# Six gate strips of layer 1 as block products in pairs, in a two-layer encoder trunk

## The chip, the cores and the metric

The kernel runs on one core of one Trainium2 chip. Its time is the device time of one execution in microseconds (us). The engines are TensorE (PE, its weight loads PEld), VectorE (DVE), ScalarE (ACT), GpSimd (POOL), and SyncE (SP), which issues nearly all DMAs from one queue in program order.

## What is computed

A trunk of two layers over 1024 tokens of width 1024. Layer 0 is differential attention, layer 1 latent attention (MLA), each with adaptive norm, a gate path `silu(z)` and a gated residual. Of the reference, what bears on the change:

```python
shift, scale, gate = _modulation(c, ada_w[i], ada_b[i])   # silu(c) @ ada_w + ada_b, in three
h = _rmsnorm(x, norm_g[i]) * (1.0 + scale) + shift
...
proj = h @ w_in                                            # layer 1
q_a, c_kv, k_pe, z = jnp.split(proj, [384, 640, 704], axis=-1)
q = (_rmsnorm(q_a, q_a_norm_g) @ w_q_b)                    # 8 heads x (128 + 64)
kv = (_rmsnorm(c_kv, kv_a_norm_g) @ w_kv_b)                # 8 heads x (128 + 128): k_nope, v
q_pe, k_pe = rope(...)
sc = (qn @ k_nope.T + qp @ k_pe.T) * scale
o = softmax(sc) @ v
o = o * silu(z)
x = x + gate * (o @ w_out)
```

z is 1024 wide: eight strips of 128 columns, one for each head.

## The kernel before

Activations lie transposed: 128 features on the partitions, 512 tokens (a half) in a row, so h1, the input of layer 1, is eight blocks k of two halves. Every operand is split into a high part (fp32r) and the rest, and each product is three matmuls (`mm3`, L178 to L180): hi x hi, lo x hi, hi x lo.

A strip (128 output columns) takes its weights as two raw tiles (`wraw`, two buffers, 256 KB each), has them split by a cast on ScalarE (L223, `wh`) and a subtraction on GpSimd (L224, `wl`), and runs two halves of 8 blocks x 3 matmuls into an accumulator of PSUM (`acc`, two buffers). Layer 1 runs 14 strips of `w_s1`: the rope part of the keys, three for q_a, two for c_kv (`lora`), then eight gate strips z (`z1_strip`). The blocks of h1 for half 0 and half 1 are made by `h_chunk` (a transposition trh on TensorE, L487 on ScalarE, L491 and L492 on VectorE), those of half 1 from a list `side`, of which one entry runs per block step of a strip.

`lora` keeps the raw strips in `craw`, sums their squares (`csum`, L1237), and `norm` adds the sums over partitions by four small matmuls (`cps`, L1242), takes the inverse root, broadcasts it through memory (`bc_s`), and scales (L1251); the results CQ and CK (hi and lo, 20 tiles) stay in SBUF. The parts of a norm are queued in `norms` and run in the next half's fifth block step.

A gate half goes from `acc` through tanh on ScalarE (L705, `zth`) and a product on VectorE (L706, `gz`) to memory, `zS`. Amid the gate strips stand eight dot products on VectorE (L428, 128x1024) of ada rows of 512 KB each, which make layer 1's gate vector.

Then come the v tiles (`v1_tile`): 16 products of CK with `wv` into `vps`, evacuated by ScalarE and VectorE as `v_hl` (L355, L356), and written to `vS` by DMAs of 512 KB. Among them stand the first strips of `stream1`, made from CQ and CK: `qr` (rope part of the queries, through `rp_sw` DMAs), `kn` and `qn`. The first scores (L1397) need all of these. Attention 1 runs head by head: scores, the maximum (L393, `nm`), exp (L395), transpositions `tr` (L376) with their two parts `pth` (ScalarE, L378) and `ptl` (VectorE, L379), and the products with v (`pv`).

The order of the instructions within an engine is a scheduler's, from the program's order and priorities.

Of the kernel before, what the change touches and what calls it, by code (L numbers as in the profile page):

```python
# [21 lines left out]
P = 128  # L22
# [56 lines left out]
def f32v(ap):  # L79
    return ap.bitcast(F32)  # L80
# [3 lines left out]
def trunk(ctx: ExitStack, tc: tile.TileContext, A, out):  # L84
# [325 lines left out]
    def mod_load(src, mp, nb, tag="ada"):  # L410
        w = mp.tile([P, D], F32, name="ada", tag=tag, bufs=nb)
        SP.dma_start(w, src)
        return w
# [56 lines left out]
                else:  # L470
                    V.tensor_scalar(piece, piece, y[:, j : j + 1], None, op0=ALU.mult)

    def h_chunk(l, xn4, k, dst, hp, sub=G, wide=False, act=False):

        _, _, _, a_, b_ = mods[l]
        if wide:
            tr = bank("cb", "trc", [P, D])[:, :HF].rearrange("p (j q) -> p j q", j=4)
        else:
            tr = bank("tr", "trh", [P, 4, P])
        for j in range(len(xn4)):  # L480
            nk = KT // len(xn4[j])
            PE.transpose(tr[:, j, :], xn4[j][k // nk][:, (k % nk) * P : (k % nk + 1) * P], ident)
        n = len(xn4)
        hh, hl = dst
        ak, bk = a_[:, k : k + 1], b_[:, k : k + 1]
        tmp = hp.tile([P, n, P], F32, name="h32", tag="h32", bufs=2)
        S.activation(hh, tr[:, :n, :], AF.Identity, bias=bk, scale=ak)  # L487
        if act:
            S.activation(tmp, tr[:, :n, :], AF.Identity, bias=bk, scale=ak)
        else:  # L490
            V.tensor_scalar(tmp, tr[:, :n, :], ak, bk, op0=ALU.mult, op1=ALU.add)  # L491
        return sub.tensor_sub(hl, tmp, f32v(hh)).ins  # L492
# [668 lines left out]
    w4 = []  # L1161

    def strip1(i, wpool=None):
        return load_strip([A["w_s1"][i, f] for f in range(2)], [4, 4], wpool)
# [1 line left out]
    def group0(gi, fulls):  # L1166
        fulls = [[x_] for x_ in fulls]
        norm_x(ss1[gi], fulls, (2, 3) if gi else ())

        def chunk(k):  # L1170
            if gi == 1:
                h1[k][1] = xt2k("h1h"), xt2k("h1l")
            h_chunk(1, fulls, k, h1[k][gi], p3x, V)
# [14 lines left out]


    stC = ExitStack()  # L1190
    cqp = pool(stC, "cq", side="right")
    CQ = [[(cqp.tile([P, HF], F32R, name=f"cqh{k}_{f}"), cqp.tile([P, HF], F32R, name=f"cql{k}_{f}")) for f in range(2)] for k in range(3)]
    CK = [[(cqp.tile([P, HF], F32R, name=f"ckh{k}_{f}"), cqp.tile([P, HF], F32R, name=f"ckl{k}_{f}")) for f in range(2)] for k in range(2)]
# [4 lines left out]
    st4 = ExitStack()  # L1198

    def kp_half(half, acc):  # L1200
        rot, fin = rope(wp, acc, half, 1.0)

        def g():
            rot()
            r = fin()
            hi = lr.tile([P, HF], F32R, name="kp_h", tag="kp_h", bufs=1)
# [4 lines left out]
        return g  # L1211

    norms = []

    def half_and_norm(w, half, consume):

        for k, _ in enumerate(gen_half(w, h1, half, consume)):
            if k == NORM_AT:
                for f in norms[:]:
                    norms.remove(f)  # L1220
                    f()

    def lora(idx, dst, gvec, width, ws=None, first=None):
        n = len(idx)
        craw = [[None, None] for _ in range(n)]
        sums = [None, None]
        def put(i, half, acc):
            t = lr.tile([P, HF], F32, name="craw", tag="craw", bufs=6)
            S.copy(t, acc)
            craw[i][half] = t  # L1230
            if i == 0:
                sums[half] = lr.tile([P, HF], F32, name="csum", tag="csum", bufs=2)
                S.activation(sums[half], acc, AF.Square)
            else:
                s2 = lr.tile([P, HF], F32, name="csq", tag="csq", bufs=1)
                S.activation(s2, acc, AF.Square)
                V.tensor_add(sums[half], sums[half], s2)  # L1237

        def norm(half):
            pt = bank("tr", "cps", [P, 4, P])  # L1240
            for j in range(4):
                PE.matmul(pt[:, 0, j : j + 1], sums[half][:, j * P : (j + 1) * P], ones[:, 0:1], start=True, stop=True)  # L1242
# [3 lines left out]
            _, rb = bcast_rows(lr, y, "cbc", 1)  # L1246
# [22 lines left out]
    def first_halves(put):  # L1269

        g0 = kp_half(0, strip_half(w4[0], h1, 0))
        for _ in gen_half(w4[1], h1, 0, put):
            side.tick()
        side.flush()
        st3x.close()
        g0()
        kp_half(1, strip_half(w4[0], h1, 1))()

    lora((1, 2, 3), CQ, qag, QL, w4[1], first_halves)
    lora((4, 5), CK, kvg, KVL)  # L1280

    def z1_strip(h, extra=None):
        w = strip1(6 + h)
        if extra:
            extra()
        for half in range(2):
            def put(acc, half=half):
                gz = silu_gate(wp, acc)
                SP.dma_start(zS[h, half], gz)
            half_and_norm(w, half, put)  # L1290

    z1_strip(0)
    stL.close()
    stv = ExitStack()
    pv1 = pool(stv, "pv1", side="right")
    p4 = pool(st4, "p4")

    c2, c_fin = load_c(p4, p4.tile([P, D], F32, name="cth", tag="ada", bufs=2))
    c_fin()
    gates = gen_gate(1, lambda src: mod_load(src, p4, 2), c2)  # L1300
    next(gates)
    wk = [[None, None] for _ in range(2)]

    def load_wk(fh, wpool):
        for k in range(2):
            raw = p4.tile([P, HF], F32, name="wvr", tag="wvr", bufs=2)
            SP.dma_start(raw, A["w_v1"][k, fh])
            h_ = wpool.tile([P, HF], F32R, name="wvh", tag="wv1", bufs=4)
            l_ = wpool.tile([P, HF], F32R, name="wvl", tag="wv1", bufs=4)
# [12 lines left out]
    for h in range(1, NH):  # L1322
        next(gates)
        z1_strip(h, lambda: [load_wk(fh, wpool) for fh, wpool in enumerate((p4, pv1))] if h == NH - 1 else None)
    for tt in range(NT):
        v1_tile(tt, 0, p4)
    st4.close()
    sth.close()

# [44 lines left out]
    for h in range(NH):  # L1374
# [4 lines left out]
    stream1 = Stream(gen_strips(items))  # L1379

    def scores1(h, half, ti, zz):

# [21 lines left out]
    def attn1(h, fills, extra=None, late=None):  # L1404
# [5 lines left out]
        def close(half, o_, zz):  # L1410
            if late and half == 1:
                ctx_["late"] = late(o_, zz, ctx_["gz"])
                return
            o = ap.tile([P, HF], F32, name="o1", tag="o", bufs=2)
            V.scalar_tensor_tensor(out=o, in0=o_, scalar=0.5, in1=ctx_["gz"], op0=ALU.mult, op1=ALU.mult)
            V.reciprocal(zz, zz)
            finish(o, zz, 1, h, half, None, ap, None)

        ctx_ = dict(pool=ap, l=1, h=h, open=open_, close=close)
        for qp in range(4):  # L1420
# [37 lines left out]
    for tt in v1_left:  # L1458
        v1_tile(tt, 1, ap, "pt", 6)
    stv.close()  # L1460
    for h in range(NH - 1):
        attn1(h, lambda i: FILL1[i])
        while late_q:
            late_q.pop(0)()
        stream1.step(sum(steps1[: h + 2]) - stream1.count)
    stw.close()
    stC.close()
    stO = ExitStack()
# [158 lines left out]
```

## Time and profile before

| what | value |
|---|---|
| median of 3 runs | 1448.29 us (1446.67 to 1448.92) |
| the profiled execution | 1448.22 us |
| its span | 1446.4 us |
| VectorE, instructions | 1272 |
| ScalarE / GpSimd, instructions | 1258 / 484 |
| layer 1's strips | 781 to 949 us |
| v tiles, to the first scores | 949 to 986 us |
| attention 1 | about 1000 to 1360 us |

The page gives an engine's busy time, its share of the span and its instructions. A row of the timeline has start, duration, engine, line, operation, output and inputs, shapes, and in brackets how long the engine had been idle and who released it. A row of the waits names who waited for whom: total, times and longest. A row of the windows has for each engine the busy time and instructions, then the granted TensorE clock (1.00 is full), the share of DMA and its rate.

### The profile page before, as it was taken

To read this page: it belongs to the slowest core of one execution; us is meant where nothing else is said; L and a number is where in the kernel's file an instruction comes from. 1 tells how busy PE (TensorE), PEld (TensorE's weight loads), DVE (VectorE), ACT (ScalarE), POOL (GpSimd) and SP (SyncE) were. 2 spreads that over 40 slices of the span, in tenths; PEclk is the share of its full clock that TensorE was granted. 3 is DMA by queue.
4 is the path that set the end of the run, shared out by engine and by line. 5 is a ranking of instruction groups with operands and counts; after the bars stand their busy time and mean duration, and the time that the engine had idled before them with its cause. 6 is when DMAs were issued, how large, how long until landed. Compare 5 with 4: busy or idle time off the path is not lost.

```text
span 1446.4 us, 20456 instructions
## 1 busy us (share of the span) xinstructions
PE 1396.9 (97%) x7424; PEld 1167.0 (81%) x7424; DVE 858.4 (59%) x1272; ACT 710.5 (49%) x1258; POOL 605.0 (42%) x484
## 2 busy tenths in 40 slices
PE   5999999999999999998999999998999999999997
PEld 4778788888888887887787878787888888888886
DVE  6656777767777767677344445134555555555365
ACT  5522366656565665566343332234454554545342
POOL 4416164656564655453551264321141321412473
PEclk9999999999999999999999999999999999999999
DMA  9787823333333324137653127367242332345574
GB/s 327 234 248 234 256 66 97 87 103 81 101 97 88 98 81 110 63 95 262 229 171 124 38 69 239 110 189 204 77 104 77 110 99 76 105 136 175 172 238 149
DMA packets 128470, 203.19 MB, mean 140 GB/s; under 512 B 18289, under 2 KB 55281, under 8 KB 128369
## 3 DMA queue, kind: packets, MB, share of 16 engines
q1 hardware_dynamic: 128368, 201.89, 45.6%
q8 instruction: 58, 0.95, 0.3%
q14 instruction: 44, 0.35, 0.1%
HBM read 132.68 MB, written 45.56 MB: 123 GB/s over the span
## 4 chain that ended last, share of the span: by engine, by line
PE 77%; DMA 7%; DVE 6%; ACT 3%; POOL 3%; issue 2%; SPq 2%; ACTq 0%; DVEq 0%; POOLq 0%
PE s L1397 10%; PE acc L180 8%; PE acc L179 8%; PE acc L178 8%; PE tr L376 7%; PE s L767 7%; PE pv L179 4%; PE pv L178 4%; PE pv L180 4%; PE oacc L178 4%; PE oacc L179 4%; PE oacc L180 4%; DMA ada<-in_ada_g 2%; DMA wvr<-in_w_v 2%; DMA vS<-v_hl 1%
## 5 line engine op out<-in xcount | busy, mean ns | idle before, releaser
L378 ACT CAST pth<-tr 128x512 fp32r<-128x512 f32 x256 | 150.3, 587 | 283.6 <-PE tr L376 280.0
L393 DVE TENSOR_REDUCE nm<-s 128x1 f32<-128x1024 f32 x192 | 234.0, 1219 | 73.6 <-PE s L767 64.0
L379 DVE TENSOR_TENSOR ptl<-tr,pth 128x512 fp32r<-128x512 f32 x256 | 176.2, 688 | 150.2 <-ACT pth L378 149.9
L224 POOL TENSOR_TENSOR wl<-wraw,wh 128x512 fp32r<-128x512 f32 (+2 forms) x94 | 116.8, 1244 | 243.4 <-ACT wh L223 216.2
L395 ACT ACTIVATE e<-s,nm 128x1024 f32<-128x1024 f32 x128 | 143.7, 1122 | 28.1 <-DVE nm L393 27.6
L376 PE MATMUL tr<-ident,e 128*128 128x128 f32 x1024 | 154.6, 273 | 1.9 <-DVE ptl L379 1.7
L376 PEld LDWEIGHTS tr<-ident,e 128*128 128x128 f32 x1024 | 121.5, 140 | 42.8 <-DVE ptl L379 19.2
L178 PE MATMUL acc<-h0h,wh 128*128 128x512 f32 x360 | 150.0, 417 | 2.0 <-DVE v_hl L356 1.9
L178 PE MATMUL pv<-pth,vt 128*128 128x256 f32 x512 | 147.4, 288 | 0.0
L179 PE MATMUL pv<-ptl,vt 128*128 128x256 f32 x512 | 145.5, 284 | 0.0
L180 PE MATMUL pv<-pth,vt 128*128 128x256 f32 x512 | 144.6, 282 | 0.0
L180 PE MATMUL acc<-h0h,wl 128*128 128x512 f32 x360 | 142.2, 395 | 0.5 <-POOL wl L224 0.5
L179 PE MATMUL acc<-h0l,wh 128*128 128x512 f32 x360 | 141.4, 393 | 0.0
L1007 POOL TENSOR_TENSOR wol<-wor,woh 128x512 fp32r<-128x512 f32 x64 | 85.8, 1361 | 84.4 <-ACT woh L1006 79.4
L178 PEld LDWEIGHTS pv<-pth,vt 128*128 128x128 f32 x512 | 97.6, 191 | 3.0 <-ACT pth L378 0.4
L179 PEld LDWEIGHTS pv<-ptl,vt 128*128 128x128 f32 x512 | 97.7, 191 | 2.6
L180 PEld LDWEIGHTS pv<-pth,vt 128*128 128x128 f32 x512 | 97.7, 191 | 0.1
L325 POOL TENSOR_TENSOR rp_sw<-rp_sw,sinT 128x512 f32<-128x512 f32 x42 | 55.2, 1314 | 80.6 <-DMA rp_sw<-rp_raw 77.6
L767 PE MATMUL s<-ks,qa 128*128 128x512 f32 x256 | 82.2, 402 | 3.5 <-DVE e L775 3.1
L775 DVE SCALAR_TENSOR_TENSOR e<-s,z,e 128x1024 f32<-128x1024 f32 x64 | 82.1, 1283 | 2.1
L223 ACT CAST wh<-wraw 128x512 fp32r<-128x512 f32 (+2 forms) x94 | 55.2, 587 | 55.8 <-PE acc L179 38.5
L320 POOL TENSOR_TENSOR rp_r<-rp_raw,cosT 128x512 f32<-128x512 f32 x38 | 49.4, 1302 | 78.5 <-ACT rp_raw L315 50.8
(469 smaller groups left out, 3281.7 us busy)
## 6 DMA issues: line engine op xcount, KB each, us to landing
wraw<-in_w_s SPq DMA_DIRECT2D x76, 256.0 KB, 2.8
ada<-in_ada_ss SPq DMA_DIRECT2D x32, 512.0 KB, 6.1
vS<-v_hl SPq DMA_DIRECT2D x32, 512.0 KB, 4.9
vt<-vS SPq DMA_DIRECT2D x32, 512.0 KB, 4.0
wor<-in_w_out SPq DMA_DIRECT2D x64, 256.0 KB, 3.9
rp_sw<-rp_raw SPq DMA_DIRECT2D x168, 64.0 KB, 2.0
bc_s<-bc_d SPq DMA_DIRECT2D x34, 256.0 KB, 4.0
ada<-in_ada_g SPq DMA_DIRECT2D x16, 512.0 KB, 5.2
```

Source lines behind the costliest of these rows:

```text
L178: PE.matmul(psum, ah, bh, start=first, stop=False)
L179: PE.matmul(psum, ah, bl, start=False, stop=False)
L180: PE.matmul(psum, al, bh, start=False, stop=last)
L224: sub = (V if pair_of else G).tensor_sub(l_[:, :n], raw[:, :n], f32v(h_[:, :n]))
L376: PE.transpose(tr[:, j, :], p[:, kt * P : (kt + 1) * P], ident)
L378: mk["S"] = S.copy(pth[kh][:, :, dst], tr).ins
L379: mk["V"] = V.tensor_sub(ptl[kh][:, :, dst], tr, f32v(pth[kh][:, :, dst])).ins
L393: mk["V"] = V.reduce_max(nm, s_ps, axis=AX.X, negate=True).ins
L395: mk["S"] = S.activation(e, s_ps, AF.Exp, bias=nm, scale=1.0, accum_out=zs).ins
L767: PE.matmul(s_ps[:, kc * HF : (kc + 1) * HF], src[:, c, ql], KS[h][kc][:, c, :], start=fst, stop=not fst)
L1007: in_turn(G.tensor_sub(lo, raw, f32v(hi)))
L1397: PE.matmul(s_ps[:, kc * HF : (kc + 1) * HF], lhs, rhs(kc), start=i == 0, stop=i == 4)
```

## The change

The gate strips 0 and 1 stay as they were. Strips 2 to 7 are taken in pairs (`z_pair`). The pair's weights are a 2 x 2 matrix of blocks (strip m, half f of the features), h1 a 2 x 2 matrix (blocks k and k + 4, half of the tokens), and the four blocks of the result come from seven products of 4 blocks x 3 matmuls (`product`, accumulator `zacc`), instead of eight, with sums ahead of and behind them:

- `combos` makes T1 to T4 of h1 on VectorE: for each k four combinations, 6 additions or subtractions and 4 subtractions for the low parts, and 4 casts on ScalarE. They are entries of `side`. h1's half 1 is kept in f32 (`h1f`) for it, and its chunks come in the order 0, 4, 1, 5, 2, 6, 3, 7.
- `z_weights` makes four sums of raw weights per pair on VectorE and splits seven tiles (ScalarE, GpSimd); raw weights come into six buffers `zraw`.
- `z_pair` adds the products up on VectorE (`zu`, `zu3`, one copy on ScalarE), with tanh and gate product as before.

For the room in SBUF, CQ and CK are written to memory (`cS`, 20 tiles of 256 KB) when they are made, and loaded again (`load_ck`) in the last pair, when T2, T3 and T1 come free. The gate vector's dot products move into attention 1 (`gate_steps`), as 16 halves of 512, with loads of 256 KB. The first `qr` weights are fetched and split ahead of the v tiles.

The core of the diff:

```diff
@@ group0 / lora
-            side.add(*[lambda k=k: chunk(k) for k in range(KT)])
+        side.add(*[lambda k=k: chunk(k) for k in ((0, 4, 1, 5, 2, 6, 3, 7) if gi else range(KT))])
...
-                    hi, lo = dst[i][half]
+                    pl, tag = (wp, "rp") if dst else (p4, "zraw")
+                    hi = pl.tile([P, HF], F32R, name="c_h", tag=tag, bufs=6)
                     S.copy(hi, t)
-                    G.tensor_sub(lo, t, f32v(hi))
-
+                    G.tensor_sub(t.bitcast(F32R), t, f32v(hi))
+                    his.append(hi)
+                norms.append(store)
+
+            def store():
+                for i in range(n):
+                    SP.dma_start(cS[dst + i, half, 0], f32v(his[i]))
+                    SP.dma_start(cS[dst + i, half, 1], craw[i][half])
@@ combos
+        for k in range(4):
+            (ah, al), (bh, bl) = h1[k][0], h1[k + 4][0]
+            c_, d_ = h1f[k], h1f[k + 4]
+            t1 = tmp4("t1")
+            V.tensor_sub(t1, c_, f32v(ah))
+            V.tensor_sub(t1, t1, f32v(al))
+            split_t(1, k, t1, t1d[k])
+            yield
+            t2 = tmp4("t2")
+            V.tensor_sub(t2, d_, t1)
+            split_t(2, k, t2, t2d[k])
+            yield
+            t4 = tmp4("t4f")
+            V.tensor_sub(t4, f32v(bh), t2)
+            V.tensor_add(t4, t4, f32v(bl))
...
+            t3_ = tmp4("t3")
+            V.tensor_sub(t3_, d_, c_)
+            split_t(3, k, t3_, (ut("t3h"), ut("t3l")))
+            yield
@@ first_halves
+        cg = combos()
+        for _ in range(16):
+            side.add(None, None, lambda: next(cg), None, None)
@@ z_weights
+            s1 = p4.tile([P, HF], F32, name="zs1", tag="zraw", bufs=6)
+            V.tensor_add(s1, a21, a22)
+            V.tensor_sub(a21, a11, a21)
+            V.tensor_sub(a11, s1, a11)
+            V.tensor_sub(a12, a12, a11)
+            for t in (a11, a21, s1, a22, a12):
+                yield split_raw(t, 4)
@@ z_pair
+        S.copy(u, product(h1q(0, 0)))
+        acc = product(h1q(1, 0))
+        c_ = rpt("z11")
+        V.tensor_add(c_, acc, u)
+        gate_out(2 * p, 0, c_, c_)
+        V.tensor_add(u, product(TC[2]), u)
+        late(0)
...
+        acc = product(TC[3])
+        u3 = rpt("zu3")
+        V.tensor_add(u3, acc, u)
+        late(1)
+        acc = product(TC[1])
+        c_ = rpt("z22")
+        V.tensor_add(c_, acc, u3)
+        V.tensor_add(u, acc, u)
+        gate_out(2 * p + 1, 1, c_, c_)
+        late(2)
...
+        V.tensor_add(u3, product(TC[4]), u3)
+        gate_out(2 * p + 1, 0, u3, u3)
+        V.tensor_add(u, product(h1q(1, 1)), u)
+        gate_out(2 * p, 1, u, u)
@@ late_z
+        if i == 0:
+            load_ck(CK, 3, [(k, half) for half in range(2) for k in range(2)])
...
+        if i == 2:
+            load_wk(0)
+            load_ck(CQ, 0, [(i, half) for half in range(2) for i in range(3)])
+    z_pair(1)
+    load_wk(1)
+    z_pair(2)
+    z_pair(3, late_z)
+    wqr0 = split_strip(kraw)
@@ gate_steps
+        for j in range(KT):
+            yield
+            for i in range(2):
+                SP.dma_start(gw[i], A["ada_g1"][j, :, i * HF : i * HF + HF])
+            yield
+            yield
+            js = slice(j, j + 1)
+            for i in range(2):
+                with behind("V"):
+                    mod_dot(gw[i], part("ada_bg1")[:, js] if i == 0 else gcol1[:, js], gcol1[:, js], cg2[i])
@@ attention 1
-        attn1(h, lambda i: FILL1[i])
+        attn1(h, lambda i: FILL1[i], lambda i: next(gate1, None))
```

How the instructions stand. On VectorE, where h1's last blocks of half 1 and the first csum are made, before:

```order
L491 TENSOR_SCALAR h_7955<-trh,moda_92,modb_93 128x512
L492 TENSOR_TENSOR h1l<-h_7955,h1h 128x512
L491 TENSOR_SCALAR h_7969<-trh,moda_92,modb_93 128x512
L492 TENSOR_TENSOR h1l<-h_7969,h1h 128x512
L491 TENSOR_SCALAR h_7987<-trh,moda_92,modb_93 128x512
L492 TENSOR_TENSOR h1l<-h_7987,h1h 128x512
L329 TENSOR_TENSOR rp_r<-rp_r,rp_sw 128x512
L1237 TENSOR_TENSOR csum<-csum,csq 128x512
```

The same place in the change (t_8008 and t_8028 are T1 and T2 of k = 0, t4f its T4):

```order
L491 TENSOR_SCALAR h1f_7931<-trh,moda_92,modb_93 128x512
L492 TENSOR_TENSOR h1l<-h1f_7931,h1h 128x512
L1243 TENSOR_TENSOR t_8008<-h1f_7861,h_0h 128x512
L491 TENSOR_SCALAR h1f_7945<-trh,moda_92,modb_93 128x512
L1244 TENSOR_TENSOR t_8008<-t_8008,h_0l 128x512
L492 TENSOR_TENSOR h1l<-h1f_7945,h1h 128x512
L1248 TENSOR_TENSOR t_8028<-h1f_7875,t_8008 128x512
L491 TENSOR_SCALAR h1f_7963<-trh,moda_92,modb_93 128x512
L1252 TENSOR_TENSOR t4f<-h_4h,t_8028 128x512
L492 TENSOR_TENSOR h1l<-h1f_7963,h1h 128x512
L1228 TENSOR_TENSOR t1l<-t_8008,t1h 128x512
```

Four combinations have moved in ahead of the last h1l; the others follow, and csum stands among them.

On SP, at the passage from the gate strips to the v tiles, before:

```order
L202 DMA wraw<-in_w_kn 128x256
L202 DMA wraw<-in_w_qn 128x384
L1408 DMA gz_9534<-zS 128x512
L1289 DMA zS<-gz 128x512
L358 DMA vS_0_71<-v_hl 256x4x128 x8
L319 DMA rp_sw<-rp_raw 32x512 x8
```

And in the change, from the last loads of CQ (L1462) on:

```order
L1462 DMA ckh<-cS 128x512
L1462 DMA ckl<-cS 128x512
L1395 DMA zS<-zu_9149 128x512
L1395 DMA zS<-zu 128x512
L358 DMA vS_0_71<-v_hl 256x4x128 x8
L202 DMA wraw<-in_w_kn 128x256
L319 DMA rp_sw<-rp_raw 32x512 x4
L202 DMA wraw<-in_w_qn 128x384
L319 DMA rp_sw<-rp_raw 32x512 x4
```

The loads from cS stand ahead of the eight vS writes, and the kn and qn weights now behind them.

On VectorE in attention 1, head 0, second half, in the change:

```order
L379 TENSOR_TENSOR ptl<-tr,pth 128x4x128
L428 ISA gwh,gcol<-gwh,c2h,vec 128x512
L428 ISA gcol 128x1
L428 ISA gwh,gcol<-gwh,c2h,gcol 128x512
L428 ISA gcol 128x1
L379 TENSOR_TENSOR ptl<-tr,pth 128x4x128
L393 TENSOR_REDUCE nm<-s_9905 128x1
L1539 SCALAR_TENSOR_TENSOR qn_l<-acc,qn_h 128x512
```

A pair of dot products and their reads stands between two ptl; before, two ptl followed each other there.

More of the change, by code (lines that the diff above doesn't have):

```diff
@@ L1190, in trunk, with ut @@
     stC = ExitStack()
[L1191 to L1193 removed]
+    up = pool(stC, "u", side="right")
+    def ut(name, spare=False, dt=F32R):
+        return up.tile([P, HF], dt, name=name, tag="us" if spare else "u", bufs=4 if spare else 20)
+    TC = {}
+    cS = dr.tile([5, 2, 2, P, HF], F32, name="cS")
     stw = ExitStack()
@@ L1295, in trunk, with z_weights @@
     pv1 = pool(stv, "pv1", side="right")
[L1296 to L1301, printed above, removed]
+    def z_weights():
+        for _ in range(1, NH // 2):
+            a11, a12 = zraw[:2]
+            yield split_raw(a11, 4)
+            yield split_raw(a12, 4)
+            a21, a22 = zraw[2:4]
+            del zraw[:4]
+            s1 = p4.tile([P, HF], F32, name="zs1", tag="zraw", bufs=6)
[5 more added lines that the diff above has]
+                yield split_raw(t, 4)
@@ new lines, in gate_out, with product @@
+    def gate_out(h, half, c_, dst):
+        th = wst.tile([P, HF], F32, name="zth", tag="gz", bufs=3)
+        S.activation(th, c_, AF.Tanh, scale=0.5)
+        V.scalar_tensor_tensor(out=dst, in0=th, scalar=1.0, in1=c_, op0=ALU.add, op1=ALU.mult)
+        SP.dma_start(zS[h, half], dst)
+    zw = z_weights()
+    zq = [next(zw), next(zw)]
+    def product(rhs):
+        hi, lo = zq.pop(0)
+        zq.append(next(zw, None))
+        acc = bank("acc", "zacc")
+        for k in range(4):
+            mm3(acc, hi[k], lo[k], *rhs[k], k == 0, k == 3)
+        return acc
@@ L1320, in v1_tile, with load_ck, late_z @@
         store_v(1, sp, acc, tt, fh, *buf)
-    for h in range(1, NH):
-        next(gates)
-        z1_strip(h, lambda: [load_wk(fh, wpool) for fh, wpool in enumerate((p4, pv1))] if h == NH - 1 else None)
+    CK, CQ = [[None, None] for _ in range(2)], [[None, None] for _ in range(3)]
+    def load_ck(dst, n0, order):
+        for i, half in order:
+            dst[i][half] = ut("ckh"), ut("ckl")
+            for j, t in enumerate(dst[i][half]):
+                SP.dma_start(f32v(t), cS[n0 + i, half, j])
+    kraw = []
+    def late_z(i):
+        if i == 0:
+            load_ck(CK, 3, [(k, half) for half in range(2) for k in range(2)])
+            raw = p4.tile([P, HF], F32, name="zraw", tag="zraw", bufs=6)
+            SP.dma_start(raw[:, : 3 * P], A["w_qr"][0])
+            kraw.append((raw, 3))
+        if i == 2:
[6 more added lines that the diff above has]
+    wqr0 = split_strip(kraw)
+    st4.close()
+    p4 = pool(st4, "p4v")
     for tt in range(NT):
```

114 lines of the change are left out of this document (87 added, 27 removed).

## The prediction

> **What bounds the kernel now.** I read the page's engine row first, then the waits of TensorE around the changed stage, then that stage cut into pieces of 20 us.
>
> ```profile
> PE 1396.9 (97%) x7424; PEld 1167.0 (81%) x7424; DVE 858.4 (59%) x1272; ACT 710.5 (49%) x1258; POOL 605.0 (42%) x484
> ```
>
> TensorE is busy for 97% of the span, so a matmul that goes is worth its own time wherever TensorE doesn't wait. The waits between 780 and 1000 us, the stretch that the change rewrites (columns: total, times, longest):
>
> ```profile
> PE vps L178 <- DVE qn_l L1349: 4.4, 1, 4.4
> PE acc L180 <- POOL wl L224: 1.5, 1, 1.5
> PE trh L482 <- DVE xfull L471: 1.5, 2, 0.8
> PE cps L1242 <- DVE csum L1237: 1.1, 1, 1.1
> ```
>
> That is 8.5 us in all. The same stretch by pieces (columns: PE, PEld, DVE, ACT, POOL busy, granted clock, DMA share, GB/s):
>
> ```profile
> 781.00:858.00 77.00, 74.36 (x347) 59.57 (x346) 35.42 (x47) 31.82 (x53) 30.99 (x23) 1.00 0.23 72
> 858.00:949.00 91.00, 89.46 (x392) 72.60 (x391) 29.93 (x42) 22.18 (x38) 32.13 (x25) 1.00 0.48 155
> 949.00:966.00 17.00, 17.00 (x75) 13.78 (x74) 6.22 (x9) 6.73 (x13) 1.17 (x2) 1.00 0.84 244
> 980.00:1000.00 20.00, 17.29 (x69) 13.91 (x70) 8.85 (x13) 8.90 (x16) 2.52 (x2) 0.83 0.86 245
> ```
>
> In the strips (781 to 949) TensorE is the bound, the other engines have half their time free, and DMA is light. In the v tiles (from 949) DMA is the busy resource. After 1000 us TensorE again works alone:
>
> ```profile
> 1000.00:1360.00 360.00, 359.53 (x2187) 308.64 (x2186) 191.59 (x257) 184.56 (x335) 99.19 (x80) 1.00 0.37 108
> ```
>
> The profiled execution took 1448.22 us (span 1446.4 and 1.8 outside it); the median of the runs is 1448.29, so sums made on the one hold for the other.
>
> **The change part by part.**
>
> *The products.* A plain strip is 2 halves x 8 blocks x 3 = 48 matmuls of 128x512, a pair 96. The pair by seven products is 7 x 4 x 3 = 84. Three pairs: 36 matmuls fewer. Their price comes from ScalarE's tanh of the second halves, three strips apart:
>
> ```profile
> 916.59 0.59 ACT L705 ACTIVATE zth<-acc 128x512 f32<-128x512 f32 x1
> ...
> 949.66 0.59 ACT L705 ACTIVATE zth<-acc 128x512 f32<-128x512 f32 x1
> ```
>
> 33.07 us for 144 matmuls is 0.2297 us each; 36 of them are **-8.3 us**. What would eat this is a product that comes late. Each lasts 12 x 0.2297 = 2.76 us. VectorE has per pair 4 sums of weights, 7 sums of products and 4 gate products, 15 x 0.69 = 10.4 us in 19.3 us, of which before's gz products were already some. ScalarE has 7 weight casts, a copy and 4 tanh at 0.6 us, GpSimd 7 weight subtractions of about 1.3 us. All stay near half load, and the scheduler puts the weights' sums two products ahead. I cost the inside of a product at nothing; one product held up by 0.5 us at each pair's start would cost 1.5.
>
> *The raw weights.* The 1.5 us wait for wl follows from weights that landed late:
>
> ```profile
> ACT wh L223 <- DMA wraw<-in_w_s: 8.6, 3, 3.3
> L428 DVE CUSTOM_DVE_ANT_0 ada<-ada,c,vec 128x1024 f32<-128x1024 f32 x8 | 11.6, 1450 | 10.8 <-DMA ada<-in_ada_g 10.8
> ```
>
> The eight ada loads of 512 KB, amid which these weights were fetched, leave the stage with their dot products: **-1.5** (between 0 and -1.5; the weights now come through a ring of six buffers, so I take the end).
>
> *h1's combinations.* They add 40 VectorE instructions and 16 casts between the last h1 chunks and the end of the k strips. A 128x512 VectorE instruction is 0.69 us, so 27.6 us more on an engine with 35.4 of 77 us: 63 of 77 us. It fits as a mean, and not where TensorE waits in order for VectorE. Two such places exist. Four of the combinations now stand ahead of the last chunk's h1l:
>
> ```profile
> 806.98 0.81 DVE L491 TENSOR_SCALAR h<-trh,moda,modb 128x512 f32<-128x512 f32 x1
> 807.82 0.69 DVE L492 TENSOR_TENSOR h1l<-h,h1h 128x512 fp32r<-128x512 f32 x1
> 816.11 0.69 DVE L329 TENSOR_TENSOR rp_r<-rp_r,rp_sw 128x512 f32<-128x512 f32 x1 [7.60 <-POOL rp_sw L325]
> ```
>
> This h1l is 4 x 0.69 = 2.8 us later, and the 7.6 us of idle behind it become the combinations' place. The other is the four norms' csum, which cps on TensorE waits for:
>
> ```profile
> 827.64 0.69 DVE L1237 TENSOR_TENSOR csum<-csum,csq 128x512 f32<-128x512 f32 x1 [4.37 <-ACT csq L1236]
> 834.38 0.90 DVE L1237 TENSOR_TENSOR csum<-csum,csq 128x512 f32<-128x512 f32 x1 [3.49 <-ACT csq L1236]
> ```
>
> VectorE was idle when these came; now up to three combinations (2.1 us) can stand ahead of each. The norm stands 4 blocks into the next half (12 matmuls, 2.8 us), which hid all but 1.1 us of one. Bounds: 0, and 2.8 + 4 x 2.1 = 11. Nearest row is the 1.1 us wait, behind three scalings of 4.40 us in all; I take about twice that, **+2**.
>
> *Normalized c through memory.* CQ and CK are written to cS (20 x 256 KB, in a stretch with DMA at 0.23 to 0.48) and read back late: 8 loads after the third product of the last pair, 8 after the fourth, 4 after the fifth, because only then are T2, T3 and T1 free. That is 5.2 MB and four zS writes, 6.3 MB, starting 4 x 2.76 = 11 us ahead of the v tiles, all in SP's queue ahead of the eight vS writes. In before, the v tiles are paced by these writes:
>
> ```profile
> 953.62 0.59 ACT L355 CAST v_hl<-vps 128x512 fp32r<-128x512 f32 x1 [0.81 <-PE vps L180]
> 957.00 0.59 ACT L355 CAST v_hl<-vps 128x512 fp32r<-128x512 f32 x1 [2.79 <-DMA vS<-v_hl]
> ...
> 964.39 0.59 ACT L355 CAST v_hl<-vps 128x512 fp32r<-128x512 f32 x1 [1.27 <-DMA vS<-v_hl]
> ```
>
> The fourth tile waits for the first write, which lands 7.8 us into the stage (start 949.23). Where reads run alone, the trace has 376 to 418 GB/s:
>
> ```profile
> GB/s 326 411 406 385 276 73 214 329 357 219 104 167 185 228 215 184 111 376 414 352 280 13 0 164 223 137 27 104 0 0 0 0 14 262 418 363 0 0 0 0
> ```
>
> At 400 GB/s the loads end 4.7 us into the v tiles; one vS write (1.85) and its landing (about 1.6, an estimate from 4.4 us of issue to landing under load) put the fourth tile at 8.2: 0.4 us late. At 330 GB/s it is 3.7 late, at the v tiles' own 244 it is 10.4 late. Behind the tiles come the rope's DMAs and the second qn half, and there TensorE stops:
>
> ```profile
> 977.90 0.39 PE L180 MATMUL vps<-wvh,ckl 128*128 128x512 f32 x1
> 982.71 0.79 PE L178 MATMUL vps<-wvh,ckh 128*128 128x512 f32 x1 [4.42 <-DVE qn_l L1349]
> 983.30 0.63 PE L179 MATMUL vps<-wvl,ckh 128*128 128x512 f32 x1
> ...
> 989.58 0.39 PE L179 MATMUL vps<-wvl,ckh 128*128 128x512 f32 x1
> 989.81 0.39 PE L180 MATMUL vps<-wvh,ckl 128*128 128x512 f32 x1
> ```
>
> The stop is 4.4 us, and for the 17 matmul steps behind it the spacing is 0.43 rather than 0.23 us, 6.87 instead of 3.9: 3 us more. The change also puts the kn and qn weights behind the vS writes (before: ahead), which would stop TensorE about 5 us earlier in the stage; but the rope's chain ends the stage either way, so these don't add up. Bounds: -3 (the stop shrinks and the slow steps vanish) and +10.4. Nearest to the 376 to 418 row, with some contention: **+2**.
>
> The Trainium skill ("TensorE: Matmul & The Clock Gate", "HAM oscillation — how this bites in real kernels") says that an idle gap of TensorE over about 3.4 us drops its clock to half. The trace agrees: after 4.4 us the granted clock falls to 0.83 in that window, after waits of 1.5 and 1.1 it stays 1.00. By this rule, not by my sum, a stage whose one stop becomes two long ones pays the 3 us twice, and one whose stop falls under the limit pays none.
>
> *The gate's dot products.* Eight rows go into attention 1 as 16 halves. A half costs half of 1.45 us and a read of 0.08: 0.8 us, 12.9 in all on VectorE, mostly behind the ptl that precedes a pv. There VectorE waits for ScalarE:
>
> ```profile
> L379 DVE TENSOR_TENSOR ptl<-tr,pth 128x512 fp32r<-128x512 f32 x121 | 83.5, 690 | 110.8 <-ACT pth L378 110.5
> 1103.77 0.69 DVE L379 TENSOR_TENSOR ptl<-tr,pth 128x512 fp32r<-128x512 f32 x1 [3.41 <-ACT pth L378]
> ```
>
> A pair (1.6 us) fits into such a gap of 3.4. Bounds: 0, and 12.9 if TensorE's transposes wait for each. Nearest to the gap: **+0.5**.
>
> *Sum*: -8.3 - 1.5 + 2 + 2 + 0.5 = -5.3, so 1448.2 - 5.3 = **1442.9**, with the runs' median 0.07 higher: 1443.0.
>
> **The rivals.**
>
> *A. The reload collides with vS.* For it: 0.84 DMA share in the v tiles, and the 244 GB/s. Against it: reads alone reach 400, and most of the reload falls ahead of the tiles. With +10.4 rather than +2: 1451.3.
>
> *B, the slower side. The dot products hold up attention 1.* Place: VectorE between two ptl of heads 0 to 3, where tr needs the ptl before and nm the scores. It takes effect if the gap is shorter than a pair, or if a half's load lands late and VectorE stands with ptl queued behind. All 16 in full: +12.9 for +0.5, so 1455.3; it decides the sign from 5.8 us on, 45% of them. Against it: gaps of 3.4 us and DMA at 0.37.
>
> *C. The combinations clog VectorE.* Four sums and the last chunk late by most of their bound, +8 rather than +2: 1448.9. For it: 82% load in the stretch. Against: the slack of 12 matmuls. The Trainium skill ("VectorE: DVE Perf Modes", "Rules for kernel authors") speaks for this rival: it advises to keep the count of chained VectorE instructions low, and the change adds 90; the trace shows room as a mean (59% busy) and one wait of 1.1 us, so far.
>
> *D. All of it is hidden.* Nothing for the combinations, and the stop before the first scores shrinks enough for the clock to hold (-3): -8.3 - 1.5 - 3 + 0.5 = -12.3, 1435.9; only the first of the two, 1440.9.
>
> *E. The products wait for their weights or banks*, so that the 36 matmuls become idle time: 8.3 us back, 1451.2.
>
> **How the numbers follow.** Forecast (1440 to 1445.4) 0.44; D 0.14; C 0.13; A 0.15; B 0.10; E 0.04. The range 1436 to 1453 takes in D, C, A and E and cuts off most of B and the extremes. The measurement can tell about 0.2%, 2.9 us, from no change. Faster than 1445.4: forecast, D and a quarter of C, 0.61. Within: the rest of C and some 0.09 of A and E, 0.19. Slower than 1451.2: the rest of A and E, and B, 0.20.
>
> **What would show it.** Products: 84 zacc matmuls per pair at 0.23 us spacing with no wait over 0.5 us; else E. Raw weights: no wait of acc for wl near the first strips; else the ada loads weren't the cause. Combinations: waits of acc for h1l and of cps for csum together near 3 us (1.1 before). Reload: the first vps some 8 us earlier than 949.2, the fourth v_hl some 8 to 10 us behind it, one stop of 4 to 6 us ahead of the first scores and a clock near 0.85 there; a second stop for kn's wh means A. Gate: tr in attention 1 without waits for ptl over 0.5 us, and PE still about 100% busy there; otherwise B. The prediction is wrong if the v stage as a whole takes over 5 us more than before, or the strips' end isn't 8 us or more earlier with the combinations' cost counted out.

## The result and the profile after

The change is slower: 1457.4 us (median of 4 runs, 1455.74 to 1459.32) against 1448.41, a ratio of 1.0065 with a 95% interval of 1.0047 to 1.0082. The forecast was 1443.0, with a range of 1436 to 1453.

| | before | after |
|---|---|---|
| profiled execution / span | 1448.22 / 1446.4 | 1459.32 / 1457.5 |
| first v tile starts | 949.23 | 956.71 |
| from there to the first scores | 36.63 | 38.25 |
| from the first scores to the end | 460.54 | 462.54 |

The page's engine row of the change:

```profile
PE 1396.9 (96%) x7388; PEld 1166.4 (80%) x7388; DVE 917.9 (63%) x1362; ACT 727.8 (50%) x1287; POOL 627.6 (43%) x493
```

TensorE has 36 matmuls fewer in the record and the same busy time, so some of the others took longer; a matmul at a lower granted clock counts as longer busy time (0.63 rather than 0.39 us in the rows below). The waits of TensorE, first between 780 and 960 us and then from 960 to 1010, show where time was lost:

```profile
PE cps L1295 <- DVE csum L1290: 11.8, 2, 7.3
PE trh L482 <- DVE xfull L471: 1.5, 2, 0.8
...
PE acc L178 <- ACT wh L223: 3.6, 1, 3.6
PE s L1587 <- DVE qn_l L1539: 1.9, 1, 1.9
```

Two waits for csum, 11.8 us, where before had one of 1.1; the wait for wl is gone, and so are the 4.4 us ahead of the first scores, in whose place stand 3.6 for the kn weights and 1.9. The same stretches as before, and two narrow ones behind the waits (columns: PE, PEld, DVE, ACT, POOL busy, clock, DMA share, GB/s):

```profile
781.00:858.00 77.00, 71.01 (x316) 56.66 (x315) 59.31 (x76) 34.99 (x59) 29.60 (x18) 0.96 0.27 84
858.00:949.00 91.00, 83.66 (x359) 68.24 (x358) 46.85 (x63) 32.76 (x56) 46.74 (x35) 0.94 0.47 152
834.00:845.00 11.00, 10.11 (x37) 8.33 (x37) 4.07 (x6) 2.65 (x5) 3.60 (x3) 0.69 0.23 71
869.00:880.00 11.00, 10.46 (x40) 8.85 (x40) 3.44 (x6) 2.30 (x5) 4.09 (x3) 0.67 0.50 153
```

VectorE went from 35.4 to 59.3 of 77 us. Behind each wait the clock is granted at some 0.7 over 11 us. On TensorE this looks so:

```profile
834.89 1.37 PE L1295 MATMUL cps<-ones,csum 128*128 128x1 f32 x8 [4.49 <-DVE csum L1290]
836.12 0.77 PE L178 MATMUL acc<-h1h,wh 128*128 128x512 f32 x1
836.69 0.63 PE L179 MATMUL acc<-h1l,wh 128*128 128x512 f32 x1
...
842.24 0.40 PE L180 MATMUL acc<-h_1h,wl 128*128 128x512 f32 x1
...
869.54 1.84 PE L1295 MATMUL cps<-ones,csum 128*128 128x1 f32 x8 [7.34 <-DVE csum L1290]
```

From 836.69 to 842.24 there are 13 steps of 0.427 us, 2.6 us more than at 0.23; behind the second wait there are 11 such steps, 2.1 more.

**Why csum is late.** VectorE's rows ahead of the first of the two waits:

```profile
818.29 0.68 DVE L1244 TENSOR_TENSOR t<-t,h_1l 128x512 f32<-128x512 f32 x1
819.00 1.74 DVE L1248 TENSOR_TENSOR t<-h1f,t 128x512 f32<-128x512 f32 x1
820.67 0.68 DVE L1228 TENSOR_TENSOR t1l<-t,t1h 128x512 fp32r<-128x512 f32 x1
...
834.05 0.68 DVE L1290 TENSOR_TENSOR csum<-csum,csq 128x512 f32<-128x512 f32 x1
```

and GpSimd's beside them:

```profile
816.08 1.74 POOL L320 TENSOR_TENSOR rp_r<-rp_raw,cosT 128x512 f32<-128x512 f32 x1
818.90 1.30 POOL L325 TENSOR_TENSOR rp_sw<-rp_sw,sinT 128x512 f32<-128x512 f32 x1 [1.08 <-DMA rp_sw<-rp_raw]
```

A combination takes 0.68 us where GpSimd is idle (818.29) and 1.74 where it works (819.00; it ends 0.5 us after GpSimd's instruction, which ran from 818.90 to 820.20). The 40 combinations took 38.0 us in all, not the 27.6 of the forecast. The Trainium skill ("SBUF — State Buffer", "Who interferes with whom") says that a VectorE instruction with two inputs in SBUF and a GpSimd instruction that reads SBUF exclude each other; these rows agree.

Ahead of the second wait:

```profile
855.05 4.31 DVE L1304 SCALAR_TENSOR_TENSOR craw<-craw,vec,bc_s 128x512 f32<-128x512 f32 x3 [1.71 <-DMA bc_s<-bc_d]
859.28 1.79 DVE L1243 TENSOR_TENSOR t<-h1f,h_3h 128x512 f32<-128x512 f32 x1
861.11 1.67 DVE L1244 TENSOR_TENSOR t<-t,h_3l 128x512 f32<-128x512 f32 x1
...
868.70 0.69 DVE L1290 TENSOR_TENSOR csum<-csum,csq 128x512 f32<-128x512 f32 x1 [0.30 <-ACT csq L1289]
```

The three scalings and nine combinations fill VectorE from 855 to 868.4. Yet csum doesn't wait for VectorE alone: ScalarE's csq stands in its bracket. ScalarE's rows:

```profile
862.81 0.62 ACT L1227 CAST t1h<-t 128x512 fp32r<-128x512 f32 x1 [1.76 <-DVE t L1244]
864.48 0.62 ACT L1227 CAST t2h<-t 128x512 fp32r<-128x512 f32 x1 [1.05 <-DVE t L1248]
867.07 0.62 ACT L1227 CAST t4h<-t4f 128x512 fp32r<-128x512 f32 x1 [1.97 <-DVE t4f L1253]
867.59 0.58 ACT L1282 COPY craw<-acc 128x512 f32<-128x512 f32 x1
868.07 0.60 ACT L1289 ACTIVATE csq<-acc 128x512 f32<-128x512 f32 x1
```

The casts wait for VectorE, and the strip's copy and its squares stand behind the casts. So VectorE's queue reaches TensorE in two ways, the second through ScalarE. The same holds ahead of the first wait: there csq ends at 833.92, 0.1 us before csum starts.

### The profile page after: what moved, and what is told of

It is laid out like the page before. It is cut to its first block, busy times and chain, and to the rows that moved or that the text cites. A ratio compares the mean times of both kernels' runs of the same rounds, so it can differ in the third digit from the quotient of the medians.

```text
span 1457.5 us, 20649 instructions
## 1 busy us (share of the span) xinstructions
PE 1396.9 (96%) x7388; PEld 1166.4 (80%) x7388; DVE 917.9 (63%) x1362; ACT 727.8 (50%) x1287; POOL 627.6 (43%) x493
## 5 line engine op out<-in xcount | busy, mean ns | idle before, releaser
L224 POOL TENSOR_TENSOR wl<-wraw,wh 128x512 fp32r<-128x512 f32 (+2 forms) x81 | 106.8, 1321 | 210.7 <-ACT wh L223 202.2
L767 PE MATMUL s<-ks,qb 128*128 128x512 f32 x256 | 80.9, 395 | 0.0
```

The source lines that it names most:

```text
L224: sub = (V if pair_of else G).tensor_sub(l_[:, :n], raw[:, :n], f32v(h_[:, :n]))
L767: PE.matmul(s_ps[:, kc * HF : (kc + 1) * HF], src[:, c, ql], KS[h][kc][:, c, :], start=fst, stop=not fst)
```

## The experiments

Times are medians; each is read against the change's 1457.4. The kernel before ran beside each of them on the same chip (medians 1446.9 to 1448.4), and the ratios to it are in the table at the end of this section. By these ratios the gains come out up to 1.8 us other than by the medians (e2 8.4 rather than 9.0, e7 5.2 rather than 6.5, e9 3.0 rather than 4.7), so a single gain is known to within about 2 us.

### Csum's additions on GpSimd (e1)

```diff
-                V.tensor_add(sums[half], sums[half], s2)
+                G.tensor_add(sums[half], sums[half], s2)
```

> csum's six additions run on GpSimd and not on VectorE; nothing is left out. In the change VectorE has up to 14 combinations and casts ahead of a csum, and TensorE waited 4.5 and 7.3 us for csum in front of cps, with the slow clock behind each wait. Theory 'queue' (csum is late because it stands behind the combinations): these waits fall to 1.5 us or less in all, the slow clock goes with them, and the time is 1457.4 - 10.5 - about 6 for the clock = 1441 (1438 to 1445). Theory 'reload' (the loss is CK and CQ's way through memory): 1455 or more, since the v stage stays as it is. Theory 'port' (the combinations are slow because GpSimd works beside them): they stay slow, 38 us for 40, but csum no longer stands behind them, so 1441 to 1446.

Measured: 1460.5, and the waits are no shorter:

```profile
PE cps L1295 <- POOL csum L1290: 13.9, 2, 7.4
```

The theories 'queue' and 'port' missed. The "1455 or more" of 'reload' holds, but the waits say that the loss is here. The squares csq come as late as in the change, behind the casts on ScalarE (csq at 834.5 and 870.0), so moving their addition to another engine doesn't help. The theory 'queue' in its simple form fell here.

### Only the splits of h1, no sums (e2)

```diff
-            V.tensor_sub(t1, c_, f32v(ah))
-            V.tensor_sub(t1, t1, f32v(al))
-            split_t(1, k, t1, t1d[k])
+            split_t(1, k, c_, t1d[k])
...
```

> Leaves out the 24 sums and differences of h1: the T tiles are splits of blocks of h1 itself (16 VectorE instructions and 16 casts rather than 40 and 16), so z is not the reference's. Products, weights and the reload stay. Queue and port: no wait of cps over 1.5 us, 1441 (1438 to 1444), the forecast's sum without its term for the combinations. Reload: 1455 or more.

Measured: 1448.4, 9.0 us less than the change. The direction is that of 'queue', the size is short by 7. One wait for csum stays (3.2, with the slow clock behind it), and so does the v stage's loss, which the experiments after this one take apart:

```profile
PE cps L1285 <- DVE csum L1280: 3.9, 2, 3.2
```

Its cause is another one, seen on VectorE:

```profile
863.88 0.69 DVE L1373 TENSOR_TENSOR zs<-zraw 128x512 f32<-128x512 f32 x1 [6.55 <-DMA zraw<-in_w_s]
```

The first sum of raw weights for a pair waits 6.6 us for its load, with the last csum queued behind it. The change has the same order, but there this sum came only at 871.59 and found its load.

### No low weights from GpSimd in strips 2 to 7 of w_s1 (e3)

These are the second and third strip of q_a, the two of c_kv and the first two gate strips, none of the paired ones.

```diff
+        if load_strip.hi_only:
+            h_ = (wp or wst).tile([P, HF], F32R, name="wh", tag="whl", bufs=4 if wp else 6)
+            S.copy(h_[:, :n], raw[:, :n])
+            hi = [h_[:, k * P : (k + 1) * P] for k in range(nk)]
+            return hi, hi
...
```

> Leaves out GpSimd's subtraction of the low weights in strips 2 to 7 of the projection (hi weights are used in their place: the same matmuls, another product), 12 of GpSimd's 128x512 instructions between 813 and 885 us; VectorE's list is as in the change. Port: the combinations take 0.69 us in most cases, 28 to 32 us for 40 rather than 38, the first stop (4.5) vanishes, the second (7.3) halves, and the time is 1457 - 4.5 - 4 - about 4 of slow clock = 1445 (1442 to 1449). Queue without port: the stops stay within 2 us of 11.8, 1454 to 1458.

Measured: 1448.9, at the end of the range of 'port'. VectorE's list is that of the change, and the waits fall to

```profile
PE cps L1305 <- DVE csum L1300: 6.7, 2, 6.3
```

The first wait (4.5) is gone, the 40 combinations take 32.8 us rather than 38.0. So 'port' explains the first wait. The second stayed at 6.3 and wasn't halved: GpSimd's three low parts of craw still run beside the scalings and two combinations there. 'Queue' alone is ruled out (1454 or more), and 'port' is not the whole.

### Half of the reload (e4)

```diff
-            dst[i][half] = ut("ckh"), ut("ckl")
-            for j, t in enumerate(dst[i][half]):
-                SP.dma_start(f32v(t), cS[n0 + i, half, j])
+            t = ut("ckh")
+            dst[i][half] = t, t
+            SP.dma_start(f32v(t), cS[n0 + i, half, 0])
```

> Leaves out the loads of the low parts of CK and CQ (10 of 20, 2.6 of 5.2 MB; the high tile is used twice, same matmuls). Reload: the first vS write starts earlier, the fourth v_hl comes 2.6 us earlier or more, and the time falls by 4 us or more, to 1453. Queue: the v stage costs only some 3 us in all against before, so at most 3 of them come back: 1454.5 to 1457, with the waits for csum as in the change.

Measured: 1453.0, the number of 'reload'; the waits for csum stayed (12.2). The fourth v_hl came 8.4 us behind the first v tile rather than 10.4, 2.0 earlier and not 2.6. From the first v tile to the first scores it took 32.83 rather than 38.25 us. But the run doesn't isolate the bytes: with fewer loads the scheduler put the kn weights ahead of the vS writes,

```profile
949.35 0.33 SPq L202 DMA_DIRECT2D wraw<-in_w_kn  x1
...
957.23 14.00 SPq L358 DMA_DIRECT2D vS<-v_hl  x8
```

whereas in the change they came behind them:

```profile
960.56 15.42 SPq L358 DMA_DIRECT2D vS<-v_hl  x8
976.08 0.66 SPq L202 DMA_DIRECT2D wraw<-in_w_kn  x1
```

### The kn weights early (e7)

```diff
...
             kraw.append((raw, 3))
+            raw = p4.tile([P, HF], F32, name="zraw", tag="zraw", bufs=6)
+            SP.dma_start(raw[:, : 2 * P], A["w_kn"][0])
+            knraw.append((raw, 2))
...
     wqr0 = split_strip(kraw)
+    wkn0 = split_strip(knraw)
```

> Nothing is left out: the first kn weights are loaded with the qr weights ahead of the reload of CQ and split ahead of the v tiles, so they no longer stand behind the eight vS writes. Theory 'load' for the strips: the waits for csum stay at about 12 us; of the v stage's loss (some 3.6 us against before, from the first v tile to the end) the wait of 3.6 us for kn's wh goes, but the rope's chain ends the stage, so 0 to 3 us come back: 1454.5 to 1457.5. Rival (the kn weights end the stage): 3.5 us and the slow clock behind it, 1451 to 1453.

Measured: 1450.95, 6.5 us less than the change: the rival was right. The reload is whole here, and the fourth v_hl is even later behind the first tile than in the change (11.2 us rather than 10.4):

```profile
965.75 0.59 ACT L355 CAST v_hl<-vps 128x512 fp32r<-128x512 f32 x1 [6.36 <-DMA vS<-v_hl]
```

Still the stage to the first scores takes 31.59 us, 6.7 less, and TensorE has no wait over 1.6 us in it:

```profile
PE acc L178 <- DVE v_hl L356: 1.6, 1, 1.6
PE vps L178 <- DVE v_hl L356: 1.1, 1, 1.1
```

The clock stays at 1.00 there. So it was the place of the first kn weights' load (128 KB), not the reload's 5.2 MB, that cost the v stage. The load of the qn weights moved up with it (issued at 974.69 rather than 980.03), and this run doesn't tell the two apart.

### The combinations' second half later, and the casts on VectorE (e5, e6)

The first holds back k = 2 and 3 until the last csum, and keeps csum and three sums of each k in the program's order:

```diff
-        for _ in range(16):
-            side.add(None, None, lambda: next(cg), None, None)
+        for i in range(16):
+            if i == 8:
+                side.add(*[None] * 44)
+            side.add(*[None] * (2 if i < 8 else 1), lambda: next(cg), *[None] * (2 if i < 8 else 0))
...
```

> Nothing is left out: h1's combinations for k = 2 and 3 are made after the last csum (from the sixth block step of the first gate strip on) instead of amid the k and c strips, and csum and the combinations are held in the program's order on VectorE. The runs so far changed the theory: csum's lateness also goes through ScalarE, whose casts of the combinations wait for VectorE with the copies and squares of the strips queued behind them; and GpSimd's instructions beside VectorE stretch the combinations from 0.69 to some 1.75 us. Theory 'load' (VectorE is full from 805 to 838 us and again from 845 to 869, and everything behind it is late): the first wait (4.5) falls to under 2, the second (7.3) vanishes, the v tiles start some 12 us earlier, at 943 to 947, and the time is 1443 to 1447. Rival 'port' alone (only the stretching matters, not the number and place): the combinations are stretched by the same instructions of GpSimd wherever they stand, so at least half of the waits stays, 1450 to 1454.

Measured: 1464.75, outside both. The waits for csum fell only to 8.1 (4.2 still for the first), and the late combinations met the pairs: ScalarE's cast of the first pair's weights came behind the last casts (t3h at 897.0 waited 3.4 us for VectorE, wh followed at 898.3), and the loads of these weights were issued only at 895.2.

```profile
PE zacc L178 <- ACT wh L223: 9.1, 1, 9.1
PE cps L1295 <- DVE csum L1290: 8.1, 2, 4.2
```

The second takes csum and the casts from the two queues:

```diff
-        S.copy(dst[0], t)
+        V.tensor_copy(dst[0], t)
...
+                G.tensor_add(sums[half], sums[half], s2)
```

> Nothing is left out: csum's additions run on GpSimd and the 16 casts of the combinations on VectorE rather than ScalarE, so that neither the squares nor the sums stand behind a combination. With csum alone on GpSimd the waits stayed (13.9 us). Theory 'chain through ScalarE' (the squares csq stand behind casts that wait for VectorE): the waits for csum fall below 3 us in all and the time is 1443 to 1447, although VectorE has 16 instructions more. Rival (GpSimd's own queue makes csum late, or TensorE then waits for another result of VectorE): waits of 8 us or more remain, 1454 or more.

Measured: 1461.4, the rival; waits for csum of 9.2 us remain. Csq is now early (837.3 for the csum below), but csum waits in GpSimd's queue behind rq_y, which waits 7.1 us for c_w, a small instruction that stands behind the combinations in VectorE's queue:

```profile
842.05 1.19 POOL L165 TENSOR_TENSOR rq_y<-c_w,mhalf 128x4 f32<-128x4 f32 x1 [7.10 <-DVE c_w L1297]
843.21 1.26 POOL L224 TENSOR_TENSOR wl<-wraw,wh 128x512 fp32r<-128x512 f32 x1
844.43 1.26 POOL L1290 TENSOR_TENSOR csum<-csum,csq 128x512 f32<-128x512 f32 x1
```

This is a third way from VectorE's load to TensorE. Three attempts to take the load off one way or out of one stretch (e1, e5, e6) made the kernel no faster; taking instructions away (e2) did.

### No dot products in attention 1 (e8)

> Leaves out the sixteen dot products of the gate vector in attention 1 and their loads (the bias alone is stored, so the output is not the reference's). Theory: they lie in VectorE's gaps, TensorE shows no wait there, so the time stays within 0.15%, 1455.5 to 1458.5. Rival B of the prediction (they stall the transpositions): 1445 to 1450.

`range(KT)` became `range(0)` in `gate_steps`. Measured: 1455.5 (1455.4 to 1458.3), the theory's lower end. From the first scores to the end it took 461.54 rather than 462.54 us. That stretch takes 461.7 to 464.7 in the kernels that keep the dot products, so their cost is about 1 us, not clear of the scatter. Rival B, with 7 us or more, is out.

### The norms' small matmuls later, and with the early kn weights (e9, e10)

```diff
-NORM_AT = 4
+NORM_AT = 7
...
-                    norms.append(lambda half=half: norm(half))
+                    norms.append((lambda half=half: norms.append(lambda: norm(half))) if dst else (lambda half=half: norm(half)))
```

> Nothing is left out: the small matmuls cps of the q norms stand 3 blocks later (at the last block of the next half), those of the c_kv norms 11 blocks later; VectorE's and ScalarE's work is the same. Theory 'load, met by cps': csum comes as late as in the change (about 834 and 869 us), but TensorE only loses time because cps stands ahead of matmuls that need nothing of it; 2.1 and 7.6 us later the first wait is 2.4 and the second nil, the slow clock behind them goes, and the time is 1457.4 - 9.4 - about 5 = 1443 (1440 to 1448). Rival 'load, met everywhere' (VectorE and ScalarE are so late that the next thing stops TensorE instead: an accumulator that isn't copied, wh or wl, h1's sums): waits of 6 us or more in all remain between 800 and 900, 1450 or more.

> Nothing is left out: the late norms and the early kn weights together. If the two losses are independent, as the places in the trace say, the gains add: 1457.4 - 14 - 6.5 = 1437 (1433 to 1442), below the kernel before. If the late norms fail, about 1450; if the earlier end of the strips makes the reload collide with vS, 1442 to 1446.

Measured: 1452.7 and 1448.4. In the first, the waits for csum fall to one of 2.5, as expected, but about 5 us come back as waits for wl and wh of the strips and the pairs, and of 14 us expected 4.7 were gained: the rival. In the second the sum of both gains would be 1446.2 (1457.4 - 4.7 - 6.5); it came out 2.2 above that, level with the kernel before (ratio 1.0015, interval 1.0000 to 1.0029). So none of these versions with all of the work is faster than the kernel before.

### Splits only, with the kn weights early, and with the late norms (e11, e12)

> Leaves out the 24 sums and differences of h1 as e2_splits_only did (z is not the reference's), and loads the kn weights early as e7_kn_early did. If the loss of the combinations (9.0 us by e2) and that of the kn weights (6.5 by e7) are independent, 1457.4 - 9.0 - 6.5 = 1442 (1440 to 1444). If the earlier strips only meet the reload (as e10 could be read, where late norms gained 2.6 rather than 9 on top of the early weights), 1446 or more.

> As e11, and the norms' cps late as in e9, so the one wait for csum that e2 kept (3.2, behind a sum that waits for raw weights) can't stop TensorE: 1442 - 3.9 - 2 of slow clock = 1437 (1434 to 1440). In e10 TensorE met waits of 1 to 2.7 us for wl and wh in place of those for csum: theory 'VectorE's load reaches them through ScalarE and the shared port with GpSimd' expects them to vanish here, with VectorE relieved and GpSimd's work the same. Rival (they are GpSimd's and the weights' own, shown once csum is out of the way): they stay at 5 us or more, 1441 to 1445.

The edits are those above, joined. Measured: 1442.6 and 1440.4. The first is the sum of the single gains to within 1 us, so the combinations (8.3 to 9.0 us for 24 of their 40 instructions; the 16 others were never left out) and the place of the kn weights (6.5) are independent losses. In the second the waits for csum are gone, and waits for wl and wh stay at 6 us in all:

```profile
PE zacc L180 <- POOL wl L224: 3.1, 2, 1.7
PE acc L180 <- POOL wl L224: 1.9, 2, 1.1
...
PE zacc L178 <- ACT wh L223: 0.9, 1, 0.9
```

The time lies between the two expectations; the waits are the rival's: with the norms late they stay although VectorE is relieved, so in e10 too they are probably for the most part the weights' own, which no run here shows by itself.

| kernel | us | ratio to before (95%) |
|---|---|---|
| the change | 1457.4 | 1.0065 (1.0047 to 1.0082) |
| e1 csum on GpSimd | 1460.5 | 1.0090 (1.0068 to 1.0113) |
| e2 splits only | 1448.4 | 1.0007 (0.9994 to 1.0019) |
| e3 no wl | 1448.9 | 1.0002 (0.9988 to 1.0017) |
| e4 half reload | 1453.0 | 1.0038 (1.0024 to 1.0053) |
| e5 late half | 1464.75 | 1.0121 (1.0101 to 1.0141) |
| e6 casts on VectorE, csum on GpSimd | 1461.4 | 1.0093 (1.0078 to 1.0109) |
| e7 kn early | 1450.95 | 1.0029 (1.0018 to 1.0040) |
| e8 no dot products | 1455.5 | 1.0059 (1.0043 to 1.0075) |
| e9 norms late | 1452.7 | 1.0044 (1.0029 to 1.0059) |
| e10 norms late, kn early | 1448.4 | 1.0015 (1.0000 to 1.0029) |
| e11 splits only, kn early | 1442.6 | 0.9965 (0.9952 to 0.9978) |
| e12 and norms late | 1440.4 | 0.9949 (0.9931 to 0.9968) |

## Why the prediction was wrong, step by step

**The products: right.** The three pairs are 252 matmuls between these two rows, and the v tiles start at 956.71:

```profile
898.75 0.39 PE L178 MATMUL zacc<-h_0h,wh 128*128 128x512 f32 x1
...
956.48 0.39 PE L180 MATMUL zacc<-h1h,wl 128*128 128x512 f32 x1
```

57.96 / 252 = 0.2300 us each and no wait, so 36 fewer are the 8.3 us of the forecast. Rival E is out.

**The raw weights: right.** The wait of 1.5 us for wl is gone.

**H1's combinations: this step failed.** With the two gains, the v tiles should have started at 949.2 - 8.3 - 1.5 = 939.4; they started at 956.7, 17.3 us later, against +2 in the sum. The trace accounts for 16.7 in the strips: waits for csum 11.8 - 1.1 = 10.7; slow steps 2.6 + 2.1 = 4.7; the slowed cps themselves 1.37 + 1.84 - 2 x 0.95 = 1.3. The other 0.6 were there before the strips began, as their first matmul shows, before and after:

```profile
781.49 0.40 PE L178 MATMUL acc<-h_0h,wh 128*128 128x512 f32 x1
782.07 0.40 PE L178 MATMUL acc<-h_0h,wh 128*128 128x512 f32 x1
```

In the three other kernels with these strips (e4, e7, e8) the v tiles start at 953.7 to 954.5, and this first matmul at 780.1 to 780.5. So of the 2.2 to 3.0 us by which they are earlier, 1.5 to 2.0 lie ahead of the strips; from that matmul on the combinations cost 15 to 17 us in all four. The first of the two places that the forecast named, the last chunk's h1l, cost nothing: no matmul waits for h1l. The step was mis-sized at the other, csum, in three ways:
- "A 128x512 VectorE instruction is 0.69 us": 0.95 as a mean of the 40 combinations, because GpSimd ran beside some of them (e3, with less of GpSimd's work, has 0.82). A row for it was in the trace of before, a csum of 1.55 us beside GpSimd's cql:

```profile
853.30 1.55 DVE L1237 TENSOR_TENSOR csum<-csum,csq 128x512 f32<-128x512 f32 x1 [2.65 <-ACT csq L1236]
853.02 1.28 POOL L1255 TENSOR_TENSOR cql<-craw,cqh 128x512 fp32r<-128x512 f32 x1
```

- "up to three combinations (2.1 us) can stand ahead of each": it was nine for the third csum, behind scalings of 4.3 us.
- Only the way over csum itself was counted. ScalarE's and GpSimd's queues carry VectorE's lateness on (e1, e6), and the clock's price behind each wait wasn't in the bound of 11 at all.

Rival C named the mechanism, at a chance of 0.13 and with +8 where about 15 to 17 were due.

**The v stage: near in size, wrong in cause.** Forecast +2; measured 1.6 to the first scores, and 2.0 behind them. Of the latter 1.6 are seven v matmuls (78 stand ahead of the first scores, 85 before): +3.6 in all. But the forecast put it on the reload and said of the kn weights that "these don't add up" with the rope's chain. e7 shows the opposite: this one place was worth 6.5 us, and without it the stage is some 3 us shorter than before's (31.59 and seven matmuls of 0.23, against 36.63). The stop for kn's wh (3.6), which the forecast had named as the sign of rival A, came without A: rival A's late fourth tile came too (10.4 after the start, 7.8 before), but TensorE's waits for v_hl are 0.7 us in the change and 2.7 in e7.

**The gate's dot products: right**, about 1 us for +0.5, and not clear of the scatter; it is part of the 2.0 behind the first scores.

The terms as measured: -8.3 - 1.5 + 17.3 + 3.6 = +11.1, the difference of the two spans. The medians differ by 9.0; the profiled execution is the longest of the change's four.

## What to carry to other kernels

VectorE, full for some 30 us, delayed the engines whose queues held an instruction that waited for it (ScalarE in e1, GpSimd in e6). So bound such a change by the load of the stretch and by all queues that pass through it, not by the instructions ahead of one consumer. Price an instruction from rows where its neighbours run as they will run after the change: here a combination took 0.68 us alone and up to 1.79 beside GpSimd. And look where small loads end up in the issuing queue: the kn weights' 128 KB behind a burst of writes cost 5 to 6.5 us, while with them ahead of it and the reload of 5.2 MB whole the v stage was shorter than before's.

## What the runs showed of the hardware

- No single length of a stop decided whether the clock fell. In e8 it fell behind a wait of 1.9 us in the v tiles, 2.3 us from the start of one matmul to the start of the next; from the sixth matmul on the steps are 0.43 us, and the granted clock from 964 to 972 us is 0.79:

```profile
964.40 0.39 PE L180 MATMUL vps<-wvh,ckl 128*128 128x512 f32 x1
966.68 0.50 PE L178 MATMUL acc<-ckh,wh 128*128 128x512 f32 x1 [1.89 <-DVE v_hl L356]
...
968.08 0.63 PE L180 MATMUL acc<-ckh,wl 128*128 128x512 f32 x1
968.51 0.63 PE L178 MATMUL acc<-ckh,wh 128*128 128x512 f32 x1
```

  In e10 a longer wait of 2.7 us, 3.1 from start to start, left it alone:

```profile
854.18 0.50 PE L180 MATMUL acc<-h_4h,wl 128*128 128x512 f32 x1 [2.69 <-POOL wl L224]
854.52 0.39 PE L178 MATMUL acc<-h_5h,wh 128*128 128x512 f32 x1
```

  Between 800 and 1000 us of all these runs, slow steps followed every stop of 3.7 us or more from one large matmul to the next (cps, of one column, not counted), some of the stops of 2.2 to 3.1 us, and no single stop under 2.2. So the figure of about 3.4 us that the prediction quoted from the Trainium skill ("TensorE: Matmul & The Clock Gate", "HAM oscillation — how this bites in real kernels") is no lower limit here; what decides between 2.2 and 3.1 us is open.
- VectorE's two-input instructions went from 0.69 to as much as 1.79 us, and GpSimd's from 1.30 to 1.74, when they ran beside each other.
